# Layer 1's modulation vectors made on VectorE in a two-layer diffusion transformer

## The chip, the cores and the metric

The kernel runs on one core of a Trainium2 chip. The metric is the device time of one execution in microseconds (us); where several executions were timed, their median. The core's engines are named as in the profile: PE is the matrix unit (TensorE), PEld its weight loads, DVE is VectorE, ACT is ScalarE, POOL is GpSimd, and SP is the engine that issues the loads from memory (DMA).

## The reference

Two layers run over 512 latent tokens and 256 context tokens of width 1024. Layer 0 mixes tokens by neighbourhood attention, layer 1 by sliding-window attention; each is followed by an MLP of width 4096 with a squared ReLU. Before each of these four parts the tokens are normalised, scaled and shifted, and the result of each is scaled by a gate. The scales, shifts and gates are the modulation vectors: six vectors per layer and stream, made from one conditioning vector per stream.

```python
silu_c = jax.nn.silu(c)
silu_cc = jax.nn.silu(c_ctx)
...
    mod_lat = (silu_c @ ada_w[i] + ada_b[i])[:, None, :]
    mod_ctx = (silu_cc @ ada_w[i] + ada_b[i])[None, None, :]
    sh1, sc1, ga1, sh2, sc2, ga2 = jnp.split(mod_lat, 6, axis=-1)
    csh1, csc1, cga1, csh2, csc2, cga2 = jnp.split(mod_ctx, 6, axis=-1)
    u_lat = modulate(rms_norm(h_lat, g_mix[i]), sh1, sc1)
    ...
    h_lat = h_lat + ga1 * y_lat
    h_lat = h_lat + ga2 * squared_relu_mlp(
        modulate(rms_norm(h_lat, g_mlp[i]), sh2, sc2), mlp_w1[i], mlp_w2[i])
```

For one layer `ada_w[i]` is a matrix of 1024 x 6144, that is 48 tiles of 128 x 1024 (six kinds of vector, eight slices k of the conditioning vector), 512 KB each.

## The kernel before, in words

Everything is kept with features on the 128 partitions and tokens along the free dimension. All products are made to nearly full precision by splitting each operand x into a high part H and a low part L = x - H of a shorter type: ACT casts H, another engine subtracts (`split`, line 203), and PE adds the three products H.H, H.L and L.H into one PSUM bank.

Weights come through `Stream` (line 307): a load by SP into one of three raw slots, then a split of 1024 columns into one of eight slots. Loads and splits run four tiles ahead of the products. In the MLP of layer 0 the split's cast is on ACT and its subtraction on DVE (on POOL for the first chunk alone, `stream.eng`).

`mlp` (line 852) walks through 16 chunks of 256 hidden features. `mlp1(c + 1)` makes the hidden features of the next chunk (two tiles j, first the 512 latent tokens, then the 256 of context); after each, `relu2` (line 859) does a relu on ACT, a multiplication on DVE that reads the PSUM bank, a cast on ACT and a subtraction on DVE. Then `mlp2(c)` makes eight output tiles f for both streams; after each product a DVE operation adds gate times bank into h (line 947). In layer 0 the latent tiles of `mlp2` take two banks in turn and those of the context two others, so the product of tile f + 2 waits until the sum of tile f has left its bank. This hand-over from `mlp1(c + 1)` to `mlp2(c)` is called the join of the chunks below.

Beside the first MLP (layer 0) runs a side generator, `ada` (line 211), that makes the six modulation vectors of layer 1. `mlp1` advances it by four steps per chunk (lines 924 to 931), and what is left is finished after the chunk before the last (line 983). One step handles one tile x of `ada_w`: x has the slice k of the conditioning vector on the partitions, so x is multiplied by one number per partition and summed over k into an accumulator `acc` of 128 x 1024, one for the latent stream (column 0 of `s32`) and one for the context (column 1). After eight tiles, products with ones on PE sum each accumulator over the partitions, ACT copies the bank, PE transposes it and DVE adds the bias (`finish`, line 224). The tiles sit in two slots; the load of a tile is issued by SP when the slot's last reader is done.

In the kernel before, the latent product goes to ACT for even k and to POOL for odd k (into a scratch `tmp`), the context product to ACT (in place, into x itself), and both sums go to POOL. In the profile the accumulators are called R, and x and tmp are part of FA; the numbers of the conditioning vector are s.

The order of the instructions in each engine's queue is set when the kernel is built, by a planner that simulates a timeline (`schedule_with_timeline_sim`, line 1422). From line 1037 on PE is excepted: its instructions keep the order of the program through this MLP. DVE's, ACT's, POOL's and SP's are ordered by the planner, and the program's order stands only where `pinned` names their engine.

In the profile nearly all instructions have line 74, the helper through which they are all issued. They are told apart by engine, operation, tiles and shape.

Of the kernel before, what the change touches and what calls it, by code (L numbers as in the profile page):

```python
# [11 lines left out]
AF = mybir.ActivationFunctionType  # L12
# [5 lines left out]
D = 1024  # L18
# [13 lines left out]
# column and shape of the small inputs in their pack  # L32
# [4 lines left out]
class Ring:  # L37
    """Equal slots of an arena, handed out in turn."""
# [10 lines left out]
def build(nc, tc, a):  # L49
    """a: DRAM access patterns by name."""  # L50
    with ExitStack() as es:
        _build(nc, tc, a, es)


def _build(nc, tc, a, es):
    pin = set()

    def pinned(*names):
        """Adds to `pin`; returns what undoes it."""
        added = set(names) - pin  # L60
        pin.update(added)
        return lambda: pin.difference_update(added)

    class Engine:
        """An engine; while its name is in `pin`, its instructions keep the order of the program."""
# [31 lines left out]
    # one more, of either type in turn  # L97
    top, top_n = [], [0]

    def region(*parts):  # L100
        """Tiles for the parts (type, size), in the place of the earlier ones."""
        while top:
            top.pop().__exit__(None, None, None)
        tiles = []
        for dtype, n in parts:
            top_n[0] += 1
            top.append(tc.tile_pool(name=f"top{top_n[0]}", bufs=1))
            tiles.append(top[-1].__enter__().tile([128, n], dtype, name=f"R{top_n[0]}", tag="R"))
        return tiles
# [33 lines left out]
    # the small inputs, packed  # L143
# [21 lines left out]
    # silu(c), silu(c_ctx), padded to 32 columns  # L165
# [10 lines left out]
    def load(out, in_):  # L176
        """A load on the SP queue; at the start, in the order given."""
        i = sy.dma_start(out, in_)
        if strict[0]:
            tc.keep_in_program_order(i)  # L180
        return i


# [14 lines left out]
    def mm_halves(pairs, start=False, stop=False):  # L198
        """Two products [128 x 64] . mv at once, one into each half of the partitions of its sum."""
        for at, (out, st, mv) in zip((0, 64), pairs):  # L200
            pe.matmul(out[at : at + 64], st, mv, start=start, stop=stop, tile_position=(0, at))

    def split(H_, L_, x, eng=None):
        """x == H_ + L_, both of float32r."""
        s.copy(H_, x)
        (eng or v).tensor_tensor(out=L_, in0=x, in1=H_.bitcast(F32), op=ALU.subtract)
# [4 lines left out]
    def ada(layer, kinds, ring, acc, tmp, ps, depth):  # L211
        """Vectors of the six, for both streams; one step per k tile, whose load runs `depth` steps ahead.

        Products and sums by k tile on DVE (one stream) and on ACT and Pool (the other), the sum over the partitions on PE."""
# [22 lines left out]
        for i, (kind, k) in enumerate(jobs):  # L237
            x = w.pop(i)
            if k == 0:
                (g.tensor_scalar(out=acc[0], in0=x, scalar1=s32[:, k, 0:1], scalar2=None, op0=ALU.mult) if k % 2 else s.activation(acc[0], x, AF.Copy, scale=s32[:, k, 0:1]))  # L240
                s.activation(acc[1], x, AF.Copy, scale=s32[:, k, 1:2])
            else:
                (g.tensor_scalar(out=tmp, in0=x, scalar1=s32[:, k, 0:1], scalar2=None, op0=ALU.mult) if k % 2 else s.activation(tmp, x, AF.Copy, scale=s32[:, k, 0:1]))
                g.tensor_tensor(out=acc[0], in0=acc[0], in1=tmp, op=ALU.add)
                s.activation(x, x, AF.Copy, scale=s32[:, k, 1:2])
                g.tensor_tensor(out=acc[1], in0=acc[1], in1=x, op=ALU.add)
# [14 lines left out]
    def ada_pe(layer, kinds, ring, ps_of, depth):  # L261
        """Vectors of the six, for both streams; one step per k tile, whose load runs `depth` steps ahead."""
# [44 lines left out]
    class Stream:  # L307
        """Weights [128, 1024] in the order of their use: loads and splits run ahead of the products."""
# [5 lines left out]
        def fill(self, n):  # L314
            """Up to n splits beyond the ones taken."""
            while self.n < min(self.i + n, len(self.items)):
                src, u = self.items[self.n]
                r = self.raw.next()
                sy.dma_start(r, src)
                with ExitStack() as held:  # L320
                    for i in self.after:
                        held.enter_context(tc.issue_after(i))
                    split(u[:, 0:1024], u[:, 1024:2048], r, self.eng)
                self.n += 1
# [9 lines left out]
    def run(gen, n=None):  # L334
        """The next n steps of a generator, or all."""
# [15 lines left out]
    def weave(*gens):  # L351
        """Generators with their step counts, emitted at an even pace."""
# [9 lines left out]
    class Stats:  # L362
        """R = 1 / sqrt(mean of squares + eps) of n tokens, on every partition; one step per feature tile."""
# [22 lines left out]
    def modulate(h_of, R, A, sh, uH, uL, tmp, view=None, split_of=None, fs=range(KT)):  # L386
        """u = h * R * A + sh, split."""
# [23 lines left out]
    def bias_tables():  # L411
        """Relative position bias per head in DRAM: of the interior queries with the mask, of the edge queries."""
# [21 lines left out]
    def head_norm(x, sq, nh):  # L434
        """rstd per head of x [128, nh * 64]; sq is scratch. One Newton step after the table functions."""
# [11 lines left out]
    def dup_mult(nat, x, r, nh, eng=g):  # L447
        """nat[:, h, 2, 64] = x[:, h, 64] * r[:, h], twice."""
# [17 lines left out]
    def views0(p):  # L466
        """Heads 2p, 2p+1: T1 = [qH; qH], T2 = [qL; qL], KK = [kH; kL] as [128, 2, 768], V as [128, 6, 2, 64]."""
# [4 lines left out]
    # q of a tile sits 64 further on, so that the two edge halves are neighbours: [448..511 | 0..447]  # L472
    def qkv0(p):
        """Eight steps: the transposes and the splits of a tile come one tile later."""
# [9 lines left out]
        def front(t):  # L484
            if p == 0:
                ps = banks[2 + t][:, 0:384]
            else:
                ps = p_mm.next()[:, 0:384]
                # late pairs: not too far ahead of the attention of the pair before
# [61 lines left out]
    def scores(ps, T1, T2, q0, K):  # L551
        """ps[:, :n] += q . k for one set of keys (n = its width)."""
# [9 lines left out]
    def merge(out, ps, i):  # L562
        """out[64 rows of head parity i] = upper half of ps + lower half."""
# [13 lines left out]
    def head0(p, i):  # L577
        """Seven steps."""
# [13 lines left out]
        for t in range(4):  # L592
            ps = p_sc.next()
            if t == 0:
                scores(ps[:, 0:256], T1, T2, 0, Kc)
                # keys 0..127 and 384..511
# [83 lines left out]

    class Wo:
        """Output projection: h += gate * (O . W), with the sums of squares of h."""

        def __init__(self, layer, T_ctx, h_of):
            """h_of(ctx, f): the tile of h."""
# [19 lines left out]
        def early(self, bk, jobs, ks):  # L705
            """The products of the O tiles ks for some output tiles ahead of the rest; one step per tile of ks."""
# [27 lines left out]
        def rest(self, stream, bk, st_lat, st_ctx, lat_done):  # L734
# [15 lines left out]
            else:  # L750
                # one half of the tokens after the other
# [12 lines left out]
    def rows(x):  # L764
        """Tokens in row order, of a view in column order."""
# [5 lines left out]
    ada_ring = Slots(*(fr(2048 + 1024 * i, 1024) for i in range(5)), *(RX[:, 1024 * i : 1024 * i + 1024] for i in range(4)))  # L771

    def ada01(q):
        """Two feature tiles of scale and shift of the first norm; the vectors side by side in one bank."""
# [212 lines left out]
    def mlp_items(layer):  # L987
        """The weights of an MLP in the order of their use."""
# [50 lines left out]
    mlp(0, True, stream, tmp, ada(1, (1, 0, 2, 4, 3, 5), adar, (RY[:, 0:1024], RY[:, 1024:2048]), fr(7680, 1024), banks[1], 2), *st_end, between=between, after_ctx=lambda: mod_ctx(1, 0, tmp2))  # L1039
# [12 lines left out]
    # P of the blocks 1, 0, 2, 3 of an even and of an odd head  # L1052
# [7 lines left out]
    # key layout of the mask: 256 of context | previous block | own block | next block | 256 of context  # L1060
# [4 lines left out]
    # q: cos, sin by gain and scale; k: by gain. The sine goes with the other half of the pair.  # L1065
# [7 lines left out]
    def roped(ps, t, e, eng):  # L1073
        """rope(gain * rms(ps)) of 4 heads, each twice; t None: without the rotation."""
# [19 lines left out]
    def proj1(pss, ts, W, ks=range(KT)):  # L1094
        """pss[i][:, ...] = u[ts[i]] . W, feature tile by feature tile."""
# [11 lines left out]
    def back1(p_tr, nat, H_, L_, lo):  # L1107
        """The four transposes of nat, split into H_ and L_ (rows from lo)."""
# [22 lines left out]
    def kv1():  # L1131
        """Keys, values and the first four heads of queries."""
# [35 lines left out]
        # the products of a tile cover the norm, the rotation and the transposes of earlier ones  # L1168
# [28 lines left out]
    def q1(gr):  # L1197
        """Nine steps: the transposes and the splits of a tile come one tile later."""
# [13 lines left out]
    class Head1:  # L1212
        """One query head: the scores with their softmax, then P . V."""
# [7 lines left out]
        def front(self):  # L1221
            """Four steps."""
# [38 lines left out]
        def back(self):  # L1261
            """Five steps."""
# [28 lines left out]
            # the products of a block come after the transposes of the next one  # L1291
# [16 lines left out]
    # h of layer 1 before its attention, in column order; from there on it is in row order  # L1308
# [56 lines left out]
def layout(inputs):  # L1365
# [3 lines left out]
    def feat(x):  # L1369
        """[tokens, D] -> [128, D / 128, tokens]"""  # L1370
# [26 lines left out]
    # rotary tables by shape alone: token t of row order at row t // 64, column t % 64  # L1397
# [9 lines left out]
def unlayout(out):  # L1407
    """[128, KT, 512] -> [1, 512, D]"""
# [17 lines left out]
```

## Time and profile before

| What | us |
|---|---|
| Median of three runs | 1726.14 |
| The three runs | 1726.14, 1725.89, 1730.58 |
| Span of the profiled execution, first to last instruction | 1729.3 |
| PE busy | 1664.0 |
| DVE busy | 1147.3 |
| ACT busy | 808.3 |
| POOL busy | 568.8 |

The profile is of one execution; its span is 1729.3 us, 3.2 us above the median of the three runs and 1.3 us below the longest. Steps worked out from the profile are parts of that span.

How to read the profile's lines: a group of instructions is shown as line, engine, operation, what it writes `<-` what it reads, shapes, `xcount | busy us, mean ns of one | idle time of the engine just before them <- what ended it`. A line of the timeline begins with its start and its length in us; `x2` means two operations in a row, and the bracket tells the idle time before them and what ended it. A line of the waits is `who <- waited for whom: us in total, times, longest`. A line of windows is a stretch of the span with each engine's busy time in it (number of instructions in brackets), the clock granted to PE as a share of the full one, and the share and rate of the DMA engines. In names, `pq` is a PSUM bank, FA an arena of plain numbers (h, raw weights, scratch), RA and R arenas of split numbers or, for R in the middle of the kernel, also the accumulators.

### The profile page before, as it was taken

How to read it: one execution, taken by the hardware profiler on the slowest of the kernel's cores; microseconds unless marked ns; L12 is line 12 of the kernel's file. 1: busy time of each engine (PE TensorE's matmuls, PEld its weight loads, DVE VectorE, ACT ScalarE, POOL GpSimd, SP SyncE). 2: the span in 40 equal slices, each digit the busy share in tenths (PEclk: the TensorE clock that was granted, in tenths of full speed). 3: DMA queues.
4: the chain of work that ended last, by engine and by line, in shares of the span. 5: the costliest groups of instructions: out<-in, count | busy, mean ns of one | idle time of the engine just before them, and what ended most of it. 6: DMA issues, size and time to landing. Idle time of an engine off the chain costs nothing.

```text
span 1729.3 us, 25192 instructions
## 1 busy us (share of the span) xinstructions
PE 1664.0 (96%) x9554; PEld 1367.6 (79%) x9554; DVE 1147.3 (66%) x2188; ACT 808.3 (47%) x1668; POOL 568.8 (33%) x377
## 2 busy tenths in 40 slices
PE   6899999999998999999999999899999999999999
PEld 3867788887787887888888888687766988888887
DVE  5866667777467655666565656888787775555554
ACT  3656666677445343434343313556676442222220
POOL 2211111112147755749184901366551040000000
PEclk8999999999998999999999999999999999999999
DMA  9554321113124233333233311110021243232201
GB/s 312 159 179 134 121 77 45 44 52 109 38 94 155 101 114 106 128 106 122 87 119 110 122 49 62 55 44 25 13 78 63 86 158 98 97 98 96 95 30 49
DMA packets 63514, 165.63 MB, mean 96 GB/s; under 512 B 6816, under 2 KB 24608, under 8 KB 63008
## 3 DMA queue, kind: packets, MB, share of 16 engines
q1 hardware_dynamic: 63392, 164.02, 28.8%
q8 instruction: 75, 1.23, 0.3%
q14 instruction: 47, 0.39, 0.1%
HBM read 159.79 MB, written 7.34 MB: 97 GB/s over the span
## 4 chain that ended last, share of the span: by engine, by line
PE 73%; DVE 11%; POOL 6%; issue 5%; ACT 3%; DMA 2%; SPq 0%; POOLq 0%; DVEq 0%; ACTq 0%
PE pq L74 73%; DVE FA L74 5%; DVE RA L74 4%; POOL R L74 3%; POOL FA L74 2%; DMA FA<-in_ada_w_dram 2%; DVE smalls L74 2%; ACT RA L74 1%; ACT FA L74 1%; DVE R L74 1%; ACT R L74 0%; SPq L74 0%; DMA FA<-in_w_dram 0%; POOL RA L74 0%; ACT smalls L74 0%
## 5 line engine op out<-in xcount | busy, mean ns | idle before, releaser
L74 PE MATMUL pq<-RA 128*128 128x512 f32 (+3 forms) x6784 | 1282.2, 344 | 32.4 <-DVE FA L74 13.6
L74 PEld LDWEIGHTS pq<-RA 128*128 128x128 f32 x6784 | 1092.6, 192 | 193.6 <-issue 20.1
L74 ACT CAST RA<-FA 128x1024 fp32r<-128x1024 f32 (+3 forms) x299 | 230.6, 795 | 395.0 <-PE pq L74 233.8
L74 DVE TENSOR_TENSOR RA<-FA,RA 128x1024 fp32r<-128x1024 f32 (+3 forms) x265 | 300.4, 1149 | 114.2 <-ACT RA L74 109.8
L74 DVE SCALAR_TENSOR_TENSOR FA<-pq,mods,FA 128x512 f32<-128x512 f32 (+1 forms) x413 | 266.3, 662 | 159.2 <-PE pq L74 157.7
L74 POOL TENSOR_TENSOR R<-R,FA 128x1024 f32<-128x1024 f32 x84 | 221.0, 2663 | 3.8 <-ACT FA L74 1.8
L74 POOL TENSOR_TENSOR FA<-FA,smalls 128x256 f32<-128x256 f32 (+1 forms) x108 | 94.8, 880 | 362.0 <-DVE smalls L74 319.4
L74 PE MATMUL pq<-RA,R 128*128 128x512 f32 (+1 forms) x870 | 177.3, 350 | 0.6 <-DVE FA L74 0.3
L74 PEld LDWEIGHTS pq<-RA,R 128*128 128x128 f32 x870 | 143.4, 188 | 25.5 <-DVE FA L74 1.2
L74 POOL TENSOR_TENSOR FA<-FA 128x256 f32<-128x256 f32 (+2 forms) x103 | 86.5, 854 | 192.4 <-ACT FA L74 178.3
L74 PEld LDWEIGHTS pq<-ident,FA 128*128 128x128 f32 x802 | 92.4, 141 | 65.9 <-issue 49.1
L74 PE MATMUL pq<-ident,FA 128*128 128x128 f32 x802 | 134.3, 282 | 8.5 <-DVE RA L74 5.3
L74 POOL TENSOR_SCALAR FA<-FA,s 128x1024 f32<-128x1024 f32 x24 | 79.6, 3318 | 156.1 <-DMA FA<-in_ada_w_dram 127.6
L74 PE MATMUL pq<-R 128*64 128x512 f32 (+2 forms) x448 | 116.2, 471 | 3.1 <-ACT R L74 1.8
L74 ACT COPY R<-pq 128x512 f32<-128x512 f32 (+3 forms) x200 | 91.3, 476 | 40.9 <-PE pq L74 40.0
L74 POOL TENSOR_TENSOR RA<-FA,RA 128x1024 fp32r<-128x1024 f32 (+2 forms) x34 | 70.3, 2083 | 109.8 <-ACT RA L74 100.7
L74 ACT ACTIVATE FA<-FA,smalls 128x512 f32<-128x512 f32 (+1 forms) x120 | 89.2, 744 | 35.9 <-DVE smalls L74 35.0
L74 ACT ACTIVATE FA<-FA,s 128x1024 f32<-128x1024 f32 x60 | 69.0, 1151 | 78.5 <-POOL FA L74 62.7
L74 DVE SCALAR_TENSOR_TENSOR FA<-pq,FA 128x512 f32<-128x512 f32 (+1 forms) x96 | 57.1, 595 | 64.5 <-ACT FA L74 64.3
L74 ACT COPY FA<-pq 128x256 f32<-128x256 f32 (+4 forms) x130 | 55.8, 429 | 76.8 <-PE pq L74 70.9
L74 ACT ACTIVATE FA<-pq 128x512 f32<-128x512 f32 (+1 forms) x96 | 49.8, 520 | 83.2 <-PE pq L74 83.2
L74 ACT ACTIVATE FA<-FA 128x256 f32<-128x256 f32 (+1 forms) x131 | 59.2, 457 | 42.0 <-DVE FA L74 32.9
(78 smaller groups left out, 985.2 us busy)
## 6 DMA issues: line engine op xcount, KB each, us to landing
FA<-in_w_dram SPq DMA_DIRECT2D x128, 512.0 KB, 3.7
FA<-in_ada_w_dram SPq DMA_DIRECT2D x80, 512.0 KB, 3.8
FA<-in_wqkv_dram SPq DMA_DIRECT2D x32, 384.0 KB, 3.6
FA<-in_wo_dram SPq DMA_DIRECT2D x16, 512.0 KB, 3.5
FA<-in_ada_w_dram SPq DMA_DIRECT2D x20, 256.0 KB, 7.6
FA<-in_wq_dram SPq DMA_DIRECT2D x8, 512.0 KB, 3.5
R<-in_ada_w_dram SPq DMA_DIRECT2D x12, 256.0 KB, 6.2
FA<-in_xT_dram SPq DMA_DIRECT2D x2, 1024.0 KB, 6.3
```

Source lines behind the costliest of these rows:

```text
L74: i = f(*args, **kw)
```

## The change

In `ada`, the 48 tiles are handled by DVE alone: the first tile of a kind by one product per accumulator, each later tile by one multiply-add per accumulator, which reads x and the accumulator and writes the accumulator. The scratch `tmp` and the writing into x fall away. The rest of the diff takes comments away. What calls `ada`, its steps, its loads and the summing over the partitions stay.

```diff
-    def ada(layer, kinds, ring, acc, tmp, ps, depth):
+    def ada(layer, kinds, ring, acc, ps, depth):
...
         for i, (kind, k) in enumerate(jobs):
             x = w.pop(i)
-            if k == 0:
-                (g.tensor_scalar(out=acc[0], in0=x, scalar1=s32[:, k, 0:1], scalar2=None, op0=ALU.mult) if k % 2 else s.activation(acc[0], x, AF.Copy, scale=s32[:, k, 0:1]))
-                s.activation(acc[1], x, AF.Copy, scale=s32[:, k, 1:2])
-            else:
-                (g.tensor_scalar(out=tmp, in0=x, scalar1=s32[:, k, 0:1], scalar2=None, op0=ALU.mult) if k % 2 else s.activation(tmp, x, AF.Copy, scale=s32[:, k, 0:1]))
-                g.tensor_tensor(out=acc[0], in0=acc[0], in1=tmp, op=ALU.add)
-                s.activation(x, x, AF.Copy, scale=s32[:, k, 1:2])
-                g.tensor_tensor(out=acc[1], in0=acc[1], in1=x, op=ALU.add)
+            for a_, col in zip(acc, range(2)):
+                if k == 0:
+                    v.tensor_scalar(out=a_, in0=x, scalar1=s32[:, k, col : col + 1], scalar2=None, op0=ALU.mult)
+                else:
+                    v.scalar_tensor_tensor(out=a_, in0=x, scalar=s32[:, k, col : col + 1], in1=a_, op0=ALU.mult, op1=ALU.add)
             if k < KT - 1:
                 fetch(i + depth)
...
-    mlp(0, True, stream, tmp, ada(1, (1, 0, 2, 4, 3, 5), adar, (RY[:, 0:1024], RY[:, 1024:2048]), fr(7680, 1024), banks[1], 2), *st_end, between=between, after_ctx=lambda: mod_ctx(1, 0, tmp2))
+    mlp(0, True, stream, tmp, ada(1, (1, 0, 2, 4, 3, 5), adar, (RY[:, 0:1024], RY[:, 1024:2048]), banks[1], 2), *st_end, between=between, after_ctx=lambda: mod_ctx(1, 0, tmp2))
```

## The prediction

> **What bounds the kernel now.** I read the page first, for the engines' shares and for the operations that the change names.
>
> ```profile
> span 1729.3 us, 25192 instructions
> PE 1664.0 (96%) x9554; PEld 1367.6 (79%) x9554; DVE 1147.3 (66%) x2188; ACT 808.3 (47%) x1668; POOL 568.8 (33%) x377
> L74 POOL TENSOR_TENSOR R<-R,FA 128x1024 f32<-128x1024 f32 x84 | 221.0, 2663 | 3.8 <-ACT FA L74 1.8
> L74 POOL TENSOR_SCALAR FA<-FA,s 128x1024 f32<-128x1024 f32 x24 | 79.6, 3318 | 156.1 <-DMA FA<-in_ada_w_dram 127.6
> L74 ACT ACTIVATE FA<-FA,s 128x1024 f32<-128x1024 f32 x60 | 69.0, 1151 | 78.5 <-POOL FA L74 62.7
> FA<-in_ada_w_dram SPq DMA_DIRECT2D x80, 512.0 KB, 3.8
> ```
>
> PE is busy for 96% of the span, so only what makes PE stop or run slowly can change the time. The 84 sums and 24 of the products on POOL, and 60 of the products on ACT, are the work that the change takes away. POOL and ACT are not bounds, so their time is worth nothing by itself.
>
> Next the stage. The operations of POOL, with their first and last start (first line below), place it, so I took 540 to 1000 us by windows, the quiet 50 us behind it (the same MLP without these vectors), and four places where PE lags.
>
> ```profile
> L74 POOL TENSOR_TENSOR R<-R,FA x84: 2374/2442/3435, 546.0 to 991.8; 128x1024 f32<-128x1024 f32 x84
> ```
>
> ```profile
> core 0: us, PE busy (x) PEld busy (x) DVE busy (x) ACT busy (x) POOL busy (x), PEclk, DMA share, GB/s
> 540.00:1000.00 460.00, 447.66 (x2524) 387.15 (x2524) 291.46 (x374) 179.44 (x233) 300.18 (x108) 0.98 0.34 113
> 1000.00:1050.00 50.00, 50.00 (x288) 43.03 (x287) 26.41 (x41) 13.35 (x20) 0.00 (x0) 1.00 0.19 64
> 550.00:560.00 10.00, 8.05 (x43) 7.23 (x42) 8.16 (x7) 3.73 (x6) 9.65 (x4) 0.83 0.46 154
> 660.00:680.00 20.00, 16.79 (x81) 14.35 (x80) 13.35 (x17) 3.23 (x5) 13.52 (x5) 0.83 0.23 80
> 735.00:750.00 15.00, 12.72 (x64) 10.82 (x63) 13.01 (x14) 5.91 (x8) 14.51 (x6) 0.89 0.34 121
> 980.00:1000.00 20.00, 16.82 (x80) 14.26 (x79) 13.37 (x17) 3.77 (x6) 14.07 (x6) 0.83 0.16 53
> ```
>
> In the stage PE is idle for 460 - 447.66 = 12.3 us; in the quiet stretch it is never idle. Four places hold 1.95 + 3.21 + 2.28 + 3.18 = 10.6 us of that, and in each the granted clock (PEclk) is low as well: 10 us at 0.83, 20 at 0.83, 15 at 0.89 and 20 at 0.83 lose 1.7 + 3.4 + 1.65 + 3.4 = 10.2 us of full-speed PE. POOL is busy in all four.
>
> Then the waits of PE in that stage, and the timeline of the second and third place (DVE with its PE rows):
>
> ```profile
> PE pq L74 <- DVE FA L74: 12.3, 8, 3.2
> 660.48 2.27 DVE L74 TENSOR_TENSOR RA<-FA,RA 128x512 fp32r<-128x512 f32 x1 [0.85 <-ACT RA L74]
> 662.67 3.39 DVE L74 TENSOR_TENSOR R<-FA,R 128x1024 fp32r<-128x1024 f32 x1
> 666.32 1.13 DVE L74 SCALAR_TENSOR_TENSOR FA<-pq,mods,FA 128x512 f32<-128x512 f32 x2
> 667.37 0.41 DVE L74 TENSOR_TENSOR RA<-FA,RA 128x256 fp32r<-128x256 f32 x1
> 667.11 1.65 PE L74 MATMUL pq<-RA 128*128 128x512 f32 x3 [3.21 <-DVE FA L74]
> 735.96 1.34 DVE L74 TENSOR_TENSOR RA<-FA,RA 128x512 fp32r<-128x512 f32 x1 [2.44 <-ACT RA L74]
> 737.22 3.44 DVE L74 TENSOR_TENSOR R<-FA,R 128x1024 fp32r<-128x1024 f32 x1
> 740.58 0.74 DVE L74 SCALAR_TENSOR_TENSOR FA<-pq,mods,FA 128x512 f32<-128x512 f32 x1
> 741.38 1.22 PE L74 MATMUL pq<-RA 128*128 128x512 f32 x2 [2.28 <-DVE FA L74]
> ```
>
> All eight waits of PE end with a DVE operation that empties a PSUM bank. At 666.32 and 740.58 that operation (the sum into h, line 947) is late because two subtractions of splits ahead of it on DVE took 2.27 + 3.39 and 1.34 + 3.44 us. What they take without POOL beside them is told by the groups of the stage (first four rows) against those of the MLP of layer 1, 1410 to 1700 us, where POOL does nothing (last three):
>
> ```profile
> L74 DVE TENSOR_TENSOR RA<-FA,RA 128x1024 fp32r<-128x1024 f32 x45 | 78.3, 1761 | 11.9 <-ACT RA L74 8.5 <-PE pq L74 2.3
> L74 DVE TENSOR_TENSOR RA<-FA,RA 128x512 fp32r<-128x512 f32 x26 | 33.0, 1271 | 22.3 <-ACT RA L74 22.3
> L74 DVE TENSOR_TENSOR RA<-FA,RA 128x256 fp32r<-128x256 f32 x28 | 23.1, 829 | 13.9 <-ACT RA L74 13.9
> L74 DVE TENSOR_TENSOR R<-FA,R 128x1024 fp32r<-128x1024 f32 x6 | 14.1, 2355 | 0.3 <-ACT R L74 0.3
> L74 DVE TENSOR_TENSOR RA<-FA,RA 128x1024 fp32r<-128x1024 f32 x39 | 47.0, 1222 | 35.7 <-ACT RA L74 35.6
> L74 DVE TENSOR_TENSOR RA<-FA,RA 128x512 fp32r<-128x512 f32 x26 | 17.9, 687 | 8.9 <-ACT RA L74 8.9
> L74 DVE TENSOR_TENSOR R<-FA,R 128x1024 fp32r<-128x1024 f32 x12 | 14.5, 1220 | 9.0 <-ACT R L74 9.0
> ```
>
> The same subtraction takes 1222 ns alone and 1761 on average beside POOL. So POOL slows DVE, DVE empties banks late, PE stops, and its clock drops.
>
> **The change part by part.**
>
> Removed from POOL: 221.0 + 79.6 = 300.6 us. Removed from ACT: 69.0 us and the first tile of each kind:
>
> ```profile
> L74 ACT ACTIVATE R<-FA,s 128x1024 f32<-128x1024 f32 x12 | 13.7, 1149 | 3.8 <-DMA FA<-in_ada_w_dram 2.6 <-PE pq L74 1.2
> ACT FA L74 <- POOL FA L74: 62.7, 19, 8.5
> ```
>
> That is 82.7 us of ACT, and 62.7 us in which ACT stood waiting for POOL with casts and relus queued behind. None of it is on the path directly.
>
> Removed from DVE: the excess beside POOL. 45 x 0.54 + 6 x 1.13 + 26 x 0.58 + 28 x 0.42 (alone 0.41, the row at 667.37) = 24 + 7 + 15 + 12 = 58 us. Afterwards POOL has no work in the stage apart from a few small operations at its ends.
>
> Added to DVE: 12 products (TENSOR_SCALAR) and 84 multiply-adds (SCALAR_TENSOR_TENSOR), 128x1024, all operands in SBUF. No row has the latter at this width. The nearest are the 1222 ns above, a pair of those back to back, and the same form at 512 columns; for the former the 640-column row (the line at 607.36 is used further down):
>
> ```profile
> 607.36 1.20 DVE L74 SCALAR_TENSOR_TENSOR FA<-pq,mods,FA 128x512 f32<-128x512 f32 x2 [0.90 <-PE pq L74]
> 608.68 2.36 DVE L74 TENSOR_TENSOR RA<-FA,RA 128x1024 fp32r<-128x1024 f32 x2
> 512.89 0.74 DVE L74 SCALAR_TENSOR_TENSOR FA<-FA,amod 128x512 f32<-128x512 f32 x1
> L74 DVE TENSOR_SCALAR FA<-FA,smalls 128x640 f32<-128x640 f32 x24 | 16.4, 708 | 0.0
> ```
>
> 0.74 against 0.687 us at 512 columns puts a multiply-add 0.05 above a subtraction, so 1.27 at 1024 when alone; the pair gives 1.18 at least. I take 1.25: 84 x 1.25 = 105 us (99 to 107). The products lie between 0.7 (as at 640) and 1.13 (scaled by width): 12 x 0.9 = 11 us. Sum 116 us, 107 to 121. DVE's load: the quiet stretch has 26.41 of 50 = 53%, or 243 us of 460; with 116 that is 359 us, 78%, against 291.46, 63%, now. DVE gains work but is not full, and no single operation of it lasts over 1.3 us, where 3.4 us is common now.
>
> Gain on the path: the 12.3 us of idle and the 10.2 us of low clock, 22.5 us, if nothing is late next. [...] The rows show the clock low around stalls of 1.95 and 2.28 us, both shorter than the 3.2 us ones. [...]
>
> What is late next: the join of the chunks, where mlp2 starts. At 660 the two subtractions had an excess of (2.27 - 0.69) + (3.39 - 1.22) = 3.75 us and PE stood 3.21; at 736 (1.34 - 0.69) + (3.44 - 1.22) = 2.87 and 2.28. So without POOL the sum into h would come about 0.55 us before PE needs the bank. One multiply-add in that spot makes PE wait 1.25 - 0.55 = 0.7 us, two in a row 1.95. The stage has 14 such joins (56 steps of the vectors, four to a chunk). Elsewhere there is cover: in mlp2 DVE has 0.90 us free in each 2.1 (1.20 busy, the row at 607.36), and what doesn't fit there has mlp1, where DVE does less. I take one multiply-add at every other join: 7 x 0.7 = 5 us given back, no clock loss, since the four stalls of under 1 us (1.7 us in all) lie outside the four windows and the windows' loss is 2.2% of 460 us, all that the stage's 0.98 leaves. Bounds: 0 (none) to 14 x 1.95 = 27 us.
>
> Also added: DVE now waits for the loads of the ada weights, where POOL did. The number of loads (48, two slots, issued on SP once a slot is read) stays; the slot is freed by DVE's second operation on a tile instead of POOL's or ACT's last. Queued behind a waiting operation on DVE are the emptying of banks and the splits, and PE behind those. Bound: nothing (a load lands 3.8 us after its issue, while DVE works on the tile before and on 53% of other things) up to the third rival's price; I take 0. The sum over the partitions on PE, the copy on ACT and the transposes stay as they are and keep their place in PE's fixed order.
>
> Sum: 22.5 - 5 = 17.5 us off the profiled execution's 1729.3, that is 1711.8. That execution's span is 3.2 us above the median of 1726.14, so part of its stalls may be missing in a median run: from the median the same sum gives 1708.6. I forecast 1710.
>
> **The rivals.**
>
> First, the joins eat the gain. If DVE places both operations of a tile ahead of the sum into h at most joins (12 to 14 of them), 23 to 27 us come back: 1726 to 1731, no change that shows. For it: only 0.55 us of slack there, and DVE at 78%. Against it: at 608.68 two 1.2 us operations in a row stand right behind the sums into h and cost PE nothing, so pairs are not harmful in themselves. [...]
>
> Second, slower: DVE's head waits for a weight load. With two slots and a reload of 3.8 us against 2.5 us of work per tile, a DVE that runs the tiles as fast as they land waits at many of them. If the order on DVE counts on an earlier landing (the page has 3.8 as the median, and ACT's one wait above lasted 2.6 us), each miss of 2 us or more at a place with 0.55 us of slack costs about 1.5 us of PE and, like the 1.95 us stall, some 1.7 us of clock: 3.2 us. Seven such misses of 48 undo the 22.5; a third of them (16) give 51 - 22.5, about +29: 1755. Against it: ACT reads the first tile of each kind now and waited for its load only once.
>
> Third, the stalls have another cause (a late relu, a late weight), and stay when POOL is quiet. Then the time stays at 1726. Against it: the quiet stretch, with the same relus and weights, has no stall at all.
>
> **How the numbers follow.** About 0.3%, 5.2 us, is what a measurement can tell from no change here. Chances: the forecast 0.66, joins 0.17, the load's wait 0.14, another cause 0.03. Alone the forecast lies between 1703.6 (all 22.5 from the median) and 1716 (one multiply-add at every join, from the span). Joins and another cause count as same, except 0.04 of the joins that end above 1731 with clock loss: faster 0.66, same 0.16, slower 0.18. The range goes from 1703 to the joins' 1731 and leaves out the slower cases.
>
> **What would show it.** Right: in the stage POOL near 0 us, DVE about 78% busy, 84 new rows near 1.25 us, 1024-wide subtractions at 1.22 us, PE idle 5 us or less, clock 1.00. Wrong: waits of PE for DVE at most joins of chunks (first rival); DVE's new rows with idle time ended by the ada loads and PEclk under 0.98 (second); multiply-adds of 2 us or more, which would put DVE over 95%.

## The result and the profile after

| Kernel | median us | runs | ratio to before |
|---|---|---|---|
| before | 1726.02 | 1725.70 to 1730.58 | 1 |
| after | 1738.74 | 1735.62 to 1739.26 | 1.0064, 95% interval 1.0049 to 1.0078 |

The change made the kernel slower by 0.64%, where 1710 was forecast. The profiled execution took 1738.84 us, its span is 1737.0.

The page after, its first lines:

```profile
span 1737.0 us, 25098 instructions
PE 1665.0 (96%) x9554; PEld 1365.7 (79%) x9554; DVE 1193.2 (69%) x2284; ACT 733.6 (42%) x1596; POOL 268.8 (15%) x269
```

POOL lost 300 us of busy time and ACT 75 (the prediction removed 82.7 from it), and DVE gained 46. PE does the same work in a longer span. Next the stage in which the vectors are made, and three places inside it, by windows:

```profile
core 0: us, PE busy (x) PEld busy (x) DVE busy (x) ACT busy (x) POOL busy (x), PEclk, DMA share, GB/s
540.00:1000.00 460.00, 441.38 (x2482) 377.96 (x2481) 332.05 (x462) 103.48 (x160) 0.00 (x0) 0.99 0.35 112
880.00:900.00 20.00, 16.31 (x86) 12.93 (x86) 19.64 (x26) 0.75 (x3) 0.00 (x0) 1.00 0.45 145
625.00:640.00 15.00, 10.71 (x47) 8.88 (x46) 14.20 (x19) 2.13 (x4) 0.00 (x0) 0.79 0.55 173
950.00:970.00 20.00, 15.43 (x78) 13.29 (x78) 19.24 (x24) 2.46 (x5) 0.00 (x0) 0.83 0.48 142
```

POOL is silent, and yet PE is idle for 460 - 441.38 = 18.6 us, against 12.3 before. Over the stage DVE is busy for 332.05 of 460, 72%; in the three places it is busy for 95 to 98%, and there PE loses 12.6 of the 18.6 us. At two of them the clock is low as well (0.79 and 0.83). The groups of DVE in the stage (540 to 1010 us) and the waits of PE and DVE say what became of the prices:

```profile
L74 DVE SCALAR_TENSOR_TENSOR R<-FA,s,R 128x1024 f32<-128x1024 f32 x84 | 105.6, 1276 | 10.5 <-DMA FA<-in_ada_w_dram 10.5
...
L74 DVE TENSOR_TENSOR RA<-FA,RA 128x1024 fp32r<-128x1024 f32 x45 | 53.9, 1221 | 10.1 <-ACT RA L74 9.4
...
L74 DVE TENSOR_TENSOR RA<-FA,RA 128x512 fp32r<-128x512 f32 x26 | 17.9, 689 | 10.9 <-ACT RA L74 10.9
...
L74 DVE TENSOR_SCALAR R<-FA,s 128x1024 f32<-128x1024 f32 x10 | 7.1, 748 | 2.2 <-PE pq L74 2.2
```

```profile
PE pq L74 <- DVE FA L74: 18.6, 15, 3.5
...
DVE R L74 <- DMA FA<-in_ada_w_dram: 10.5, 8, 2.1
```

The subtractions are back at 1221 and 689 ns (1761 and 1271 before): the contention is gone. But PE now waits 15 times for a bank that DVE has to empty, and DVE itself waits 8 times for a tile of `ada_w`, 10.5 us in all. Where both meet is seen on the timeline, here round the second place, in order of time except for PE's last row, which ends the stall:

```profile
611.94 1.07 PE L74 MATMUL pq<-R,ones 128*32 128x512 f32 x8
613.35 1.41 DVE L74 TENSOR_SCALAR R<-FA,s 128x1024 f32<-128x1024 f32 x2
...
621.36 4.87 DVE L74 SCALAR_TENSOR_TENSOR R<-FA,s,R 128x1024 f32<-128x1024 f32 x4 [1.82 <-DMA FA<-in_ada_w_dram]
626.14 0.68 DVE L74 SCALAR_TENSOR_TENSOR FA<-pq,FA 128x512 f32<-128x512 f32 x1
627.63 2.48 DVE L74 SCALAR_TENSOR_TENSOR R<-FA,s,R 128x1024 f32<-128x1024 f32 x2 [0.81 <-DMA FA<-in_ada_w_dram]
630.03 1.22 DVE L74 TENSOR_TENSOR RA<-FA,RA 128x1024 fp32r<-128x1024 f32 x1
631.17 0.42 DVE L74 SCALAR_TENSOR_TENSOR FA<-pq,FA 128x256 f32<-128x256 f32 x1
631.50 0.74 DVE L74 SCALAR_TENSOR_TENSOR FA<-pq,mods,FA 128x512 f32<-128x512 f32 x1
632.30 2.99 PE L74 MATMUL pq<-RA 128*128 128x512 f32 x12 [3.24 <-DVE FA L74]
```

The products with ones at 611.94 read the accumulators and so set them free. Right behind them, at 613.35, the next kind begins. From there its 16 operations follow one another; the join of the chunks falls in the middle of them. The last of the rows on DVE is the sum into h for which PE has stood 3.24 us. Ahead of it in DVE's queue lie six multiply-adds and two waits for loads of tiles, 1.82 and 0.81 us. The groups of DVE from 613 to 650 us and the head of the next burst:

```profile
L74 DVE SCALAR_TENSOR_TENSOR R<-FA,s,R 128x1024 f32<-128x1024 f32 x14 | 17.5, 1277 | 2.6 <-DMA FA<-in_ada_w_dram 2.6
...
L74 DVE TENSOR_SCALAR R<-FA,s 128x1024 f32<-128x1024 f32 x2 | 1.4, 744 | 0.0
```

```profile
690.63 1.07 PE L74 MATMUL pq<-R,ones 128*32 128x512 f32 x8
691.73 1.42 DVE L74 TENSOR_SCALAR R<-FA,s 128x1024 f32<-128x1024 f32 x2 [1.10 <-PE pq L74]
```

All 16 operations of the kind are done by 650 us; then DVE has none of them for 40 us, until the next products with ones. Four of the six kinds go so; in the third and the fifth the two products stand right behind the products with ones too, and the 14 multiply-adds follow 10 and 27 us later, again close together. The operations do not stand where the program has their steps, four to a chunk. The work comes in six bursts, one per kind, and all 15 stalls of PE lie in these.

The kernel before had the same bursts, on POOL. Its sums of a kind stand close together, with a pause before the next kind:

```profile
546.00:594.00 48.00, 45.82 (x254) 40.05 (x253) 34.74 (x36) 22.95 (x30) 45.55 (x17) 0.96 0.37 126
595.00:622.00 27.00, 27.00 (x155) 22.66 (x154) 15.71 (x28) 7.82 (x11) 0.00 (x0) 1.00 0.31 100
```

POOL is busy for 95% of the first stretch and for none of the second. So the record before the change already showed that the steps are not spread evenly; the prediction took only the stage's first and last sum from it.

PE runs the same 9,554 matmuls in the same order in before, after and all experiments but e3, e5, e9 and e10 (there the products with ones stand elsewhere), so the start of one and the same matmul can be compared from trace to trace. "Lag" below is that start against the first experiment's (no multiply-adds), as it grows between the matmuls that stand at 540 and at 1000 us of after. It is 22.8 us for before (23.4 some matmuls later, when its last low clock is over) and 31.1 for after; after collects it in the six bursts, some 3.5, 7.3, 4.2, 2.9, 5.4 and 7.7 us.

### The profile page after: what moved, and what is told of

It is laid out like the page before. It is cut to its first block, busy times and chain, and to the rows that moved or that the text cites. A ratio compares the mean times of both kernels' runs of the same rounds, so it can differ in the third digit from the quotient of the medians.

```text
span 1737.0 us, 25098 instructions
## 1 busy us (share of the span) xinstructions
PE 1665.0 (96%) x9554; PEld 1365.7 (79%) x9554; DVE 1193.2 (69%) x2284; ACT 733.6 (42%) x1596; POOL 268.8 (15%) x269
## 4 chain that ended last, share of the span: by engine, by line
PE 79%; DVE 12%; issue 3%; DMA 3%; ACT 3%; POOL 1%; SPq 0%; DVEq 0%; POOLq 0%; ACTq 0%
PE pq L74 79%; DVE FA L74 6%; DVE RA L74 3%; DMA FA<-in_ada_w_dram 2%; DVE R L74 2%; DVE smalls L74 1%; ACT RA L74 1%; ACT FA L74 1%; POOL FA L74 0%; ACT R L74 0%; DMA FA<-in_w_dram 0%; SPq L74 0%; ACT smalls L74 0%; POOL RA L74 0%; DVE amod L74 0%
## 5 line engine op out<-in xcount | busy, mean ns | idle before, releaser
L74 DVE TENSOR_TENSOR RA<-FA,RA 128x1024 fp32r<-128x1024 f32 (+3 forms) x265 | 249.3, 955 | 91.4 <-ACT RA L74 89.6
L74 DVE SCALAR_TENSOR_TENSOR R<-FA,s,R 128x1024 f32<-128x1024 f32 x84 | 105.6, 1276 | 10.5 <-DMA FA<-in_ada_w_dram 10.5
L74 DVE SCALAR_TENSOR_TENSOR RA<-pq,cst,RA 64x128 fp32r<-64x128 f32 (+2 forms) x152 | 58.1, 383 | 24.1 <-ACT RA L74 20.6
L74 ACT ACTIVATE RA<-pq,cst 64x128 fp32r<-64x128 f32 (+2 forms) x152 | 58.7, 392 | 34.8 <-PE pq L74 18.3
```

What stands on the lines that cost most here:

```text
L74: i = f(*args, **kw)
```

## The experiments

Each ratio is to the kernel before as timed in the same session. Theories: **placement** (operations stand ahead of sums into h, in bursts; the first expectations call it bunching), **load wait** (DVE's head waits for a tile; the prediction's second rival), **load** (the work on DVE, wherever it lies), and for the kernel before **contention** against ACT waiting for POOL.

**e1_floor.** The 84 multiply-adds left out.

```diff
-                else:
+                elif k < 0:
```

> Leaves out the 84 multiply-adds (tiles k = 1 to 7 of each kind are loaded but not read), so the vectors hold the first tile's part alone. Three theories of the slower kernel: bunching (the planner puts the 16 operations of a kind on DVE within some 27 us, where DVE then has more work than time), load wait (DVE's queue stands at the load of an ada tile with bank sums behind it), load (the 116 us that DVE has more, in operations of 1.27 us, wherever they stand). All three expect PE without stalls between 560 and 1000 us: after loses 18.6 us of visible idle and 6.8 us of half clock there, some 4 to 5 us more in gaps too short to show, so 1738.7 - 30 = about 1709. If the stalls have another cause, 1726 or more.

1706.65 us, ratio 0.9887 (0.9864 to 0.991). In its windows PE is never idle and at full clock:

```profile
540.00:1000.00 460.00, 460.00 (x2663) 399.92 (x2662) 255.18 (x403) 111.74 (x173) 0.00 (x0) 1.00 0.36 116
```

As all three theories expected, PE does not stop. So before had 1.13% to gain, and after is 32 us above the floor. Its timeline of DVE at the join that was the prediction's second place shows what spare time there is; PE's row runs over it without a gap:

```profile
653.95 0.69 DVE L74 TENSOR_TENSOR RA<-FA,RA 128x512 fp32r<-128x512 f32 x1 [0.69 <-ACT RA L74]
655.57 1.22 DVE L74 TENSOR_TENSOR R<-FA,R 128x1024 fp32r<-128x1024 f32 x1 [0.93 <-ACT R L74]
656.71 0.41 DVE L74 SCALAR_TENSOR_TENSOR FA<-pq,FA 128x256 f32<-128x256 f32 x1
657.04 1.13 DVE L74 SCALAR_TENSOR_TENSOR FA<-pq,mods,FA 128x512 f32<-128x512 f32 x2
```

DVE stands idle for 0.93 us between the two subtractions, for ACT's cast. The first sum into h ends at 657.78, and the product that needs the bank starts at 658.60: 0.76 us more once the 0.06 from sum to product is taken off (632.24 to 632.30 in after). Together 1.69 us fit in here.

**e2_paced.** Each tile's two operations tied behind the DVE instruction that precedes them in the program, in the steps as they are (the third of the four right at the join, the fourth among the first sums behind it).

```diff
-            for a_, col in zip(acc, range(2)):
+            with tc.issue_after(v.last):
+                for a_, col in zip(acc, range(2)):
...
```

> Same work, but each tile's two operations may start only behind the DVE instruction that stands before them in the program, so the tiles are spread four to a chunk, one of them still at the join. Bunching: stalls of some 0.5 to 1 us at the 13 joins stay, the six bursts go: 1715 to 1722. Load: the same work, 1735 to 1739. Load wait: slots are free longer before their next use, loads land in time: 1715 to 1725 too.

1736.55 us, ratio 1.0062 (1.0043 to 1.0081). That is the range of the load theory, which e3 puts to the test. The bursts are gone and the time is not, so bunching alone, as it was put here, failed. But a part of the waits is of another kind:

```profile
PEld pq L74 <- DVE R L74: 10.0, 6, 4.6
PE pq L74 <- DVE R L74: 6.1, 3, 4.4
PE pq L74 <- DVE FA L74: 9.4, 14, 1.1
```

R are the accumulators: held back, they come late for the products with ones, whose place PE cannot change (at the worst PE stands 4.41 us, and the eight products behind it take 3.12 us, where those at 611.94 in after took 1.07). The waits for FA are those for sums into h; six of them, some 70 us apart or more, are of 1.07 to 1.12 us. This run changed two things at once and decides nothing about the bursts; the next one takes the steps to other places.

**e3_paced_off_joins.** As e2, but the four steps at the start of `mlp1`, after its first latent and first context relu, and after output tile 3 of `mlp2`; none at the join.

```diff
                 start(0)
+                run(side, 1)
                 lat(0)
...
                 lat(1)
-                run(side, 1)
                 ctx(1)
-                run(side, 1)
...
+                    if f == 3:
+                        run(side, 1)
```

> As the paced kernel, but the four steps of a chunk stand at the start of mlp1, after its first latent and first context tile, and in the middle of mlp2 (after f = 3), none at the join. Bunching: nearly no stall is left, 1709 to 1713, faster than before. Load: 1735 to 1739. Load wait: like the paced kernel, no better, 1715 to 1725.

1717.81 us, ratio 0.9953 (0.9938 to 0.9968): the same operations, now faster than before. The load theory is out. The time lies 5 us above what bunching expected; it lies in the load wait's range, but that theory expected it to be no better than e2, and it is 19 us better. DVE waits for a tile only once, for 1.3 us. Ten gaps of 0.76 to 0.80 us are left in `mlp2`; at the one of 636 us a pair of 2.47 us and two more operations stand among tiles with 0.90 us to spare.

**e4_one_slot.** The kernel after with one slot for tiles instead of two. Since two loads are still issued ahead, a step here reads the tile that was loaded after its own, so the vectors are made of other tiles.

```diff
-    adar = Ring(FA, FX + 3072, 1024, 2)
+    adar = Ring(FA, FX + 3072, 1024, 1)
```

> The change as it is, but one slot for the ada tiles instead of two: a tile is loaded (3.8 us) only when the one before has been read. Bunching: the eight tiles of a kind take 50 us instead of 27, DVE keeps room in between, stalls fall to under half: 1715 to 1727. Load wait: DVE stands at every one of the 48 loads: 1745 or more. Load: unchanged, 1735 to 1740.

1740.33 us, ratio 1.0081 (1.0053 to 1.0109), nearest to the load theory, which e3 has put out, and in neither of the other two ranges. DVE waits four times as long for loads, and PE's total of waits (21.3 us) is just 2.7 above after's:

```profile
DVE R L74 <- DMA FA<-in_ada_w_dram: 44.5, 37, 2.4
PE pq L74 <- DVE FA L74: 21.3, 19, 3.7
```

Spreading the operations by slots did not help, and load waits did not cost in proportion. So the length of DVE's waits alone does not set the loss.

**e5_singles.** As e3, but the operations one at a time: two steps at each of the three places in `mlp1`, one after output tile 2 of `mlp2` and one after tile 5.

```diff
             for a_, col in zip(acc, range(2)):
+                with tc.issue_after(v.last):
...
-            if k < KT - 1:
-                fetch(i + depth)
+                if k < KT - 1 and col:
+                    fetch(i + depth)
-                yield
+                yield
...
+                    if f in (2, 5):
+                        run(side, 1)
```

> The whole computation, with the 96 operations one at a time instead of in pairs: two at the start of mlp1, two after its first latent relu, two after its first context relu, one after output tile 2 of mlp2 and one after tile 5; none at the join. Placement theory (what costs time is an operation or a pair of them ahead of a sum into h or beside tiles of mlp2 whose spare time is 0.90 us in 2.1): the ten 0.76 us gaps that the pair left in the middle of mlp2 go, 1708 to 1713, under the 1717.8 of the version with pairs. Load theory (DVE's total of 72% in the stage costs, wherever the work lies): the same work as before, so 1717 or more.

1708.31 us, ratio 0.9905 (0.989 to 0.9919). All 96 operations are there, and the kernel is within 2 us of the floor, as placement expected. These ten gaps are gone. One product with ones waits 1.18 us, most of what is left.

**e6_pool_sums.** The kernel before, its 84 sums alone.

```diff
-                (g.tensor_scalar(out=tmp, in0=x, ...) if k % 2 else s.activation(tmp, x, ...))
-                g.tensor_tensor(out=acc[0], in0=acc[0], in1=tmp, op=ALU.add)
-                s.activation(x, x, AF.Copy, scale=s32[:, k, 1:2])
+                g.tensor_tensor(out=acc[0], in0=acc[0], in1=x, op=ALU.add)
```

> The kernel before without the products of all tiles but the first of each kind: POOL's 84 sums over 128x1024 stay (they add the unscaled tile), the products on ACT and POOL are left out. Contention theory (the kernel before loses its time because POOL's sums stretch DVE's subtractions beside them): the 84 sums alone still stretch them, 1717 to 1726. Rival (it loses it because ACT stands waiting for POOL with casts and relus queued behind): near the floor without vectors, 1706 to 1710.

1724.36 us, ratio 0.9997 (0.9985 to 1.001): as slow as before, in the range of contention, and ACT has no wait for POOL any more. The groups:

```profile
L74 POOL TENSOR_TENSOR R<-R,FA 128x1024 f32<-128x1024 f32 x84 | 226.8, 2740 | 221.8 <-DMA FA<-in_ada_w_dram 184.6 <-ACT RA L74 37.1
L74 DVE TENSOR_TENSOR RA<-FA,RA 128x1024 fp32r<-128x1024 f32 x47 | 85.9, 1850 | 16.0 <-ACT RA L74 12.3 <-PE pq L74 2.1
```

The sums alone stretch DVE's subtractions to 1850 ns and give a lag of 18.4 us. Contention is what held the kernel before; ACT waiting for POOL is not.

**e7_no_reload.** The kernel after, loading two tiles alone.

```diff
-                load(w[i], ...)
+                if i < 2:
+                    load(w[i], ...)
```

> The kernel after with only the first two of the 48 tiles loaded; all others are read from the same two slots again, so no multiply-add waits for a load (46 loads left out, the vectors are made of the wrong tiles). Placement theory (bursts of pairs ahead of sums into h): no gain, 1735 to 1742, perhaps slower since the bursts get denser. Load-wait theory (the second rival: DVE's head waits for the tile while the sums into h queue behind it): 1712 to 1725.

1729.70 us, ratio 1.0033 (1.0021 to 1.0044), between the two expectations: no wait for a load at all, and PE still waits:

```profile
PE pq L74 <- DVE FA L74: 13.8, 20, 1.4
```

The lag is 23.6 us: 7.5 of the 31.1 go.

**e8_one_stream.** The kernel after without the context vectors' multiply-adds.

```diff
-                else:
+                elif col == 0:
```

> The kernel after with the multiply-adds of the context vectors left out: 42 multiply-adds instead of 84, one per tile, the loads and the rest as they are. Load theory (loss in proportion to the work put on DVE): half of the 32 us between 1738.7 and the floor of 1706.7 stays, about 1722. Placement theory (a single operation of 1.28 us ahead of a sum costs about 0.7 us, a pair 1.95 and more, with a low clock behind it): much less than half stays, 1707 to 1714.

1728.78 us, ratio 1.0025 (1.0012 to 1.0038). Half the work is gone and the lag is 23.2 us. It fits neither expectation. The waits say why:

```profile
DVE R L74 <- DMA FA<-in_ada_w_dram: 21.8, 15, 2.3
PE pq L74 <- DVE FA L74: 14.8, 8, 3.8
```

A DVE that is sooner done with a tile waits longer for the next one (21.8 us, after 10.5), again at its queue's head. The longest stall, 3.8 us, is longer than any of after.

**e9_join_one and e10_join_two.** As e5, with one or both of the operations of the third place in `mlp1` moved behind the second latent relu, that is ahead of the sums into h at every join. The diff is e9's against e5:

```diff
                 ctx(0)
-                run(side, 2)
+                run(side, 1)
                 start(1)
                 lat(1)
+                run(side, 1)
                 ctx(1)
```

> The whole computation. As the version with single operations, but one of the two operations that followed the first context relu of mlp1 is moved behind mlp1's second latent relu and its split, which puts it on DVE ahead of the sums into h at each of the 14 joins. Placement by the price of the prediction (0.55 us of slack at the join, so 1.25 - 0.55 = 0.7 us for one operation): 14 x 0.7 = 10 us above the 1708.3 of the version with none there, 1718. Rival, that a single operation there is harmless and only bursts of several with a wait for a load cost time: 1707 to 1711.

> As the one before with both operations moved to that place, so a pair of 2.5 us ahead of the sums into h at each of the 14 joins, evenly spread, and no burst. Placement by the price of the prediction: 14 x 1.95 = 27 us above 1708.3, 1735, the loss of the changed kernel without its bursts. Rival, that it takes the burst with its waits for loads: 1707 to 1715.

One: 1705.39 us, ratio 0.9874 (0.9842 to 0.9906). Two: 1714.42 us, ratio 0.993 (0.9903 to 0.9958). The price of the prediction (1718 and 1735) fails in both; the rival's ranges hold for two, and one is even below its own. The stage of the first by windows, and a join of the second on the timeline, with its PE row:

```profile
540.00:1000.00 460.00, 460.00 (x2664) 400.00 (x2663) 345.66 (x486) 111.09 (x171) 0.00 (x0) 1.00 0.36 116
```

```profile
622.63 2.48 DVE L74 SCALAR_TENSOR_TENSOR R<-FA,s,R 128x1024 f32<-128x1024 f32 x2
625.02 1.22 DVE L74 TENSOR_TENSOR RA<-FA,RA 128x1024 fp32r<-128x1024 f32 x1
626.16 0.42 DVE L74 SCALAR_TENSOR_TENSOR FA<-pq,FA 128x256 f32<-128x256 f32 x1
626.50 2.18 DVE L74 SCALAR_TENSOR_TENSOR FA<-pq,mods,FA 128x512 f32<-128x512 f32 x4
627.29 4.92 PE L74 MATMUL pq<-RA 128*128 128x512 f32 x26 [0.30 <-DVE FA L74]
```

One operation ahead of the sums costs nothing: PE is busy for the whole 460 us, while DVE does 345.66 us, more than in after. A pair costs PE 0.30 to 0.47 us at 11 of the joins; from one to two the medians differ by 9 us, 0.65 per join, a third of the 1.95 that was forecast. The 1.69 us of the floor's timeline say the same: 1.28 fits, 2.48 doesn't. So single operations at joins, spread evenly, cost nothing and pairs little (up to 1.12 us at some joins of e2, where they stand behind the first sum), and the 31 us need something that holds up DVE for longer.

**e11_one_stream_no_reload.** The cuts of e7 and e8 together.

> The kernel after with both cuts at once: the multiply-adds of the context vectors left out (42 of 84 stay) and only the first two of the 48 tiles loaded. Each cut alone left 23 of the 31 us. If the loss is the work and the waits ahead of the same sums into h, added up (a wait of some 2 us for a load or a second operation at a join do the same harm), taking both away leaves little: 1708 to 1714. If each cut only moved the order of the operations, and any order of this kind costs about 23 us: 1725 to 1732.

1708.60 us, ratio 0.9893 (0.9861 to 0.9925), lag 1.1 us, as expected if work and waits add up ahead of the same sums. Each cut alone takes 7.5 to 8 us off, both together 30: a burst reaches across the join as long as either its own work or its loads hold it up. With neither, at the join of 622 us there is a single operation (the first row) ahead of the sum into h (the last):

```profile
620.14 1.28 DVE L74 SCALAR_TENSOR_TENSOR R<-FA,s,R 128x1024 f32<-128x1024 f32 x1
621.33 1.22 DVE L74 TENSOR_TENSOR RA<-FA,RA 128x1024 fp32r<-128x1024 f32 x1
622.47 0.42 DVE L74 SCALAR_TENSOR_TENSOR FA<-pq,FA 128x256 f32<-128x256 f32 x1
622.80 0.74 DVE L74 SCALAR_TENSOR_TENSOR FA<-pq,mods,FA 128x512 f32<-128x512 f32 x1
```

**e12_three_slots.** The kernel after with a third slot and three loads ahead.

```diff
-    adar = Ring(FA, FX + 3072, 1024, 2)
+    adar = Two(FA[:, FX + 3072 : FX + 4096], FA[:, FX + 4096 : FX + 5120], fr(7680, 1024))
...
```

> The whole computation. The kernel after with a third slot for the tiles, where the scratch of the kernel before was, and three loads in flight, so that a burst waits less for loads. Load waits as a part of the loss: like the version that loads only two tiles, 1728 to 1733. Load waits without a part: 1736 to 1741. Denser bursts, with eight tiles' pairs sooner behind one another: above 1741.

1734.55 us, ratio 1.0041 (1.0025 to 1.0058), just between the first two expectations. DVE's waits for tiles fall from 10.5 to 6.7 us, and the lag from 31.1 to 27.2. A real change of the buffers, with the order left as it is, wins a small part back.

## Why the prediction was wrong, step by step

- *POOL slows DVE, DVE empties banks late, PE stops.* Right, and shown: e6 keeps nothing of the vectors but POOL's sums and is as slow as before, with DVE's subtractions at 1850 ns (1221 in after).
- *ACT's and POOL's time is worth nothing by itself.* Right: e6 takes 60 operations of ACT and 24 products of POOL away without a gain. What POOL's sums cost, they cost by slowing DVE.
- *The price on DVE, 116 us.* Right: 84 x 1.276 + 12 x 0.748 = 116. The load of 78% came out as 72% in after and 345.66 of 460, 75%, where PE never stops (e9).
- *The gain of 22.5 us.* Right for the profiled execution: before's lag against the floor is 22.8 us. In the medians the gain is 1.13%, some 19 us, so the sum was a few us too high there, as the prediction thought possible. The low clock belonged in the sum: 8.1 of the 22.8 us grow inside it, and the 12.3 us of idle time alone don't reach the total.
- *5 us given back at the joins.* This is the step that failed; the runs showed 31. Two things were in it. The slack was taken as 0.55 us from excess less stall; it is 1.69, because DVE's wait of 0.93 us for ACT's cast takes part of a delay up (e1, e9, e10). That error was on the safe side. The other one decided: "one multiply-add at every other join" supposed the steps evenly spread, as the program has them, four to a chunk. But DVE's order is the planner's, and in it the 16 operations of a kind stand in a burst, ahead of sums into h and with waits for loads among them. Two things told of it beforehand: the program's place binds only engines that are pinned, and DVE isn't; and POOL's sums stood in six bursts in the profile of before.
- *The load's wait on DVE, taken as 0.* Wrong too. Alone it is worth some 7.5 us of the 31 (e7), and without it the smaller work would have cost next to nothing (e8 against e11). The row that served as argument (ACT waited for a load only once) was of an engine that was itself held back by POOL, which gives a load more time to land (argued; no run shows it alone). POOL's row in the first view of the prediction spoke against it: 127.6 us of its idle time ended with these loads.
- *Chances.* The rivals named the place (joins) and the wait (DVE's head), but each as a mechanism by itself, and 16 missed loads as the price of the second. Neither is what happened alone: 8 waits for loads and the bursts added up ahead of the same sums. The upper bound of 27 us for the joins was worked out from 14 pairs; a burst of six operations with waits for loads in it isn't held by it, and so the range ended too low.
- *The clock.* "No clock loss" was part of the failed step. Where after's 31.1 us come from is told by the starts of its matmuls, one by one, against the floor's. The lag grows by 21.3 us at the 15 matmuls that end a stall: 18.6 us of idle time that shows, and some 0.18 us at each that does not, since in an unbroken row the profile's end of a matmul lies beyond the next start (one ends at 665.57, the next starts at 665.40). It grows by 5.0 us inside the two spells of low clock, and by the other 4.8 us in steps of mostly 0.1 us at single matmuls in the bursts.

What stays open: how the planner came to this order (no run varied its costs), and whether e9 (1705.39) and e5 (1708.31) differ at all; their intervals overlap. Both are faster than before and after, with the changed kernel's operations in another order: the change was good, its order wasn't.

## What to carry to other kernels

When side work moves to an engine that also releases the bottleneck, its price here was not the sum of its durations but what stood behind it in the queue: the same 96 operations gave 1738.7 us in bursts and 1705.4 spread one at a time. So ask first who orders the new engine's queue, and look at the busiest 20 us rather than at the mean (the engine that did the work before may show the bursts already); 72% over the stage was 95 to 98% in the bursts. Move operations one by one behind work that has just been released, keep waits for loads away from the head of that queue, and check that a held-back result is not late for a consumer with a fixed place.

## What the hardware showed that was not expected

The clock did not follow the length of a stall alone. In after the stalls of 3.24 and 3.48 us were each followed by a low clock (the rows of 625 and 950 us above, 0.79 and 0.83), and one of 2.11 us was not (the row of 880, 1.00). In e12 a stall of 2.52 us cost clock and a longer one of 2.79 us did not; PE's rows that end the two:

```profile
629.70 1.55 PE L74 MATMUL pq<-RA 128*128 128x512 f32 x5 [2.52 <-DVE FA L74]
956.11 1.21 PE L74 MATMUL pq<-RA 128*128 128x512 f32 x4 [2.79 <-DVE FA L74]
```

The stretches round the two:

```profile
620.00:640.00 20.00, 16.87 (x91) 14.60 (x90) 20.00 (x25) 2.95 (x5) 0.00 (x0) 0.91 0.55 167
945.00:965.00 20.00, 15.85 (x91) 12.95 (x89) 19.27 (x24) 2.96 (x5) 0.00 (x0) 1.00 0.45 144
```

Round the shorter stall PE is idle for 3.13 of 20 us in all and the clock is 0.91; round the longer one it is idle for 4.15 us and the clock stays at 1.00. In before a stall of 1.95 us came with a low clock as well (550 to 560 us, 0.83), shorter than the 2.11 us that cost none in after. So in these runs neither the length of a stall nor the idle time in the 20 us round it told whether clock was lost. What decides it was not shown, and a sum built on the lengths of stalls can only bound its price.
